# A hybrid decoder layer on one core: attention sums placed between gate units, and weight loads scheduled first

## The chip, the cores and the metric

The kernel runs on one core of a Trainium2 chip, as one launch. The metric is device time in microseconds (us), the median of several runs. Engines are named as the profile does: PE (matrix multiplies), PEld (its weight loads), DVE (vector), ACT (scalar), POOL (GpSimd) and SP (which issues nearly all DMAs here).

## The reference, cut to what matters

One decoder layer over 1024 tokens of width 1024, all in float32. The part around the change:

```python
proj = h @ w_in                        # q, k, v of mLSTM and attention, gates
# attention: 3 groups (dilations 1, 4, 16), 8 heads each; outs and log-denominators
wts = jax.nn.softmax(jnp.stack(lses, axis=0), axis=0)
y_b = jnp.sum(wts[..., None] * jnp.stack(outs, axis=0), axis=0)
g_a, g_b = jnp.split(jax.nn.sigmoid(gate_pre), 2, axis=-1)
merged = g_a * (y_a @ w_proj_a) + g_b * (y_b @ w_proj_b)
x = x + merged @ w_out
x = x + (jax.nn.silu(hf @ w_gate) * (hf @ w_up)) @ w_down
```

`y_b` is a sum over the three dilations; `gate_pre` is 2048 more columns of `proj`.

## The kernel before, in words

Every large product is done as three float32r products (high times high, high times low, low times high). A weight piece is loaded into a `raw` tile by `raw_piece` (L97 to L100; two `raw` buffers, 512 KB each), and `split` (L102) makes its high part on ACT (L103) and its low part on POOL (L104). The projections use a Strassen-like scheme with seven block products: `gemm_s` (L279) calls `w7`, which loads **two** raw pieces, the upper and the lower half of the rows, and forms the four sums S1 to S4 of them on DVE (L241 to L244); only the form A11 needs the first piece alone. The seven products P1, P7, P6, P5, P2, P4, P3 then run on PE (L263 to L265), 12 matmuls of 128x512 each, so 84 for a unit. The four output blocks leave PSUM through DVE (L294, and L668 in a gate unit), a gate unit's go through a tanh on ACT (L669) and are stored to DRAM (`gt_d`, L670) from one of two `e` tiles. P7 of the next unit needs the PSUM bank that L668 of this one empties.

After the projections and the recurrence of each head, the kernel comes to the part in question. `attn_combine` stores the softmax weights of the groups (`c_d`, L637). `attn_sum(i)` (L641, i = 0 to 3) makes `y_b`: for two halves and three groups, so six iterations, it loads the weights of two heads, each broadcast over 64 partitions (L649, two DMAs), and the group's numerators (L651), multiplies them on DVE (L652), adds (L654), and stores the half to `yb_d` (L657). All these tiles are `c` tiles, of which there are six. In all there are 24 iterations. `merge_b` (L967) then reads `yb_d` back (L963), splits it on ACT and POOL and multiplies it with `w_proj_b` (L184 to L186); `merge_a` goes on with `w_proj_a`.

The order of instructions on each engine, and in the DMA queue of SP, is not that of the code: a scheduler takes the program, gives each instruction a priority by its place in it, and fixes at build time in which row each engine works. Each engine then works through its row strictly in order, and SP waits at a DMA whose buffer or data is not ready, whatever stands behind. The place in the program is set by the list `ORDER` (L915): `m` are mLSTM heads, `a` attention pairs, `r` rows of denominators, `c` the combine, `g` gate units, `s` the four sums. Gate units 8 to 11 follow the sums there.

At the start of the kernel, SP loads eight tiles of x (L77) and, between the second and the third, the first two raw pieces. ACT sums their squares (L138), DVE scales them (L149), PE transposes them (L155).

Of the kernel before, what the change touches and what calls it, by code (L numbers as in the profile page):

```python
# [19 lines left out]
P = 128  # L20
# [19 lines left out]
def layer_kernel(ctx, tc, x, norm_mix_g, w_in, b_gate_if, conv_w, conv_b, mlstm_norm_g,  # L40
# [3 lines left out]
    ACT, DVE, POOL, PE, SP = nc.scalar, nc.vector, nc.gpsimd, nc.tensor, nc.sync  # L44
# [10 lines left out]
    def T(tag, shape, dt=F32):  # L55
        cnt[0] += 1
        return sb.tile(list(shape), dt, tag=tag, bufs=SBT[tag], name=f"{tag}{cnt[0]}")

    def PS(tag, shape=(P, 512)):
        cnt[0] += 1  # L60
        return ps.tile(list(shape), F32, tag=tag, bufs=PST[tag], name=f"p{tag}{cnt[0]}")
# [34 lines left out]

    def raw_piece(src, r0, nk, c0, ncol, tag="raw"):  # L97
        raw = T(tag, (P, nk, ncol))
        SP.dma_start(raw, src[r0:r0 + nk * P, c0:c0 + ncol].rearrange("(k p) c -> p k c", p=P))
        return raw  # L100

    def split(dh, dl, src):  # L102
        ACT.activation(dh, src, AF.Copy)  # L103
        POOL.tensor_tensor(dl, src, f(dh), op=ALU.subtract)  # L104

    raw0 = [raw_piece(w_in, kp * P, 4, C_VM + (NH - 1) * DH, 264) for kp in (0, 4)]
    for t in range(2, NT):
        load_x(t)
# [59 lines left out]
    def w_tiles(src, r0, K, c0):  # L168
        res = [(T("whi", (P, K, P), F32R), T("wlo", (P, K, P), F32R)) for _ in range(2)]
        for p in range(0, K, 4):  # L170
            raw = raw_piece(src, r0 + p * P, 4, c0, 256)
            for m in range(2):
                split(res[m][0][:, p:p + 4, :], res[m][1][:, p:p + 4, :], raw[:, :, m * P:(m + 1) * P])
        return res
# [14 lines left out]
    def gemm_h(src, r0, c0, ncol, K, stat, evac, raws=None, ts=range(NT), tags=(("whi", "wlo"),) * 2, quick=False):  # L189
        pieces = []  # L190
        for kp in range(0, K, 4):
            raw = raws[kp // 4] if raws else raw_piece(src, r0 + kp * P, 4, c0, ncol)
            wh, wl = (T(tg, (P, 4, ncol), F32R) for tg in tags[kp // 4])
            if quick:
                for ks, eng in ((slice(0, 2), DVE), (slice(2, 4), POOL)):
                    ACT.activation(wh[:, ks], raw[:, ks], AF.Copy)
                    eng.tensor_tensor(wl[:, ks], raw[:, ks], f(wh[:, ks]), op=ALU.subtract)
            else:
                split(wh, wl, raw)
            pieces.append((wh, wl))  # L200
        for t in ts:
            p = PS("mm", (P, ncol))
            for k in range(K):
                wh, wl = pieces[k // 4][0][:, k % 4, :], pieces[k // 4][1][:, k % 4, :]
                sh, sl = stat(k, t)
                PE.matmul(p, sh, wh, start=(k == 0), stop=False)  # L206
                PE.matmul(p, sh, wl, start=False, stop=False)
                PE.matmul(p, sl, wh, start=False, stop=(k == K - 1))
            evac(t, p)
# [702 lines left out]
        ACT.activation(hi, t1s[k], AF.Copy)  # L912
        DVE.tensor_tensor(lo, t1s[k], f(hi), op=ALU.subtract)

    ORDER = "m0 a00 a01 r0 m1 a10 a11 r1 m2 a20 a21 r2 c m3 g0 g1 g2 g3 s0 s1 s2 s3 g8 g9 g10 g11".split()  # L915
    mlstm_gates()
    mlstm_v2(0)
    for g in range(3):
# [21 lines left out]

    for step in ORDER:
        if step[0] == "a":
# [233 lines left out]
    for B in range(NS // BK):  # L1176
# [15 lines left out]
        for cg in range(2):  # L1192
            def wpiece(half, m, tags):

                c0 = cg * 512 + m * 256
                rows = w_down[B * BK * 256:(B + 1) * BK * 256, c0:c0 + 256].rearrange("(k i p) c -> i p k c", i=2, p=P)[half]
                res, k0 = [], 0
                for tg, nk in tags:
                    t_ = T(tg, (P, nk, 256))
                    SP.dma_start(t_, rows[:, k0:k0 + nk, :])  # L1200
                    res.append((t_, slice(k0, k0 + nk)))
                    k0 += nk
                return res
            a11, a21 = wpiece(0, 0, [("raw", BK)]), wpiece(0, 1, [("raw", BK)])
            a22, a12 = wpiece(1, 1, [("u", 2), ("u", 1)]), wpiece(1, 0, [("u", 2), ("u", 1)])
            s1, s2 = T("sm", (P, BK, 256)), T("sm", (P, BK, 256))
# [75 lines left out]
    for c in range(2):  # L1282
        wd.append([])
        for k0 in range(0, K4, 2):
            raw = T("raw", (P, 2, 512))
            r0 = (2 * NS + k0) * P
# [13 lines left out]
    for t in range(NT):  # L1300
        ssq, sd = small(2), small(1)
        for c in range(2):
            p = PS("mm")
# [61 lines left out]
```

## Time and profile before

| what | value |
|---|---|
| median of 3 runs | 2164.43 us (2159.92 to 2174.46) |
| the profiled execution | 2172.26 us |
| its span, first to last instruction | 2170.3 us |
| PE busy | 2033.1 us, 94% of the span |
| POOL, DVE, ACT busy | 965.0, 1355.7, 811.3 us |
| mean granted clock of PE | 0.974 of full |

The profile is of one execution, and the times in its rows are microseconds from the start of the span. "Busy" counts the time in which an engine works at an instruction. The bracket at the end of a row of the timeline is the idle time of that engine ahead of the row, and what ended it. Names of tiles are shown without their numbers there (`raw<-in_w_in` is a load of a piece of `w_in` into a raw tile).

### The profile page before, as it was taken

The page shows a single profiled execution, that of the slowest core. Times are in us where ns is not written, and L with a number is a line of the kernel's source. Part 1 is how long each engine was busy: PE and PEld are TensorE (multiplying, and loading weights), DVE is VectorE, ACT ScalarE, POOL GpSimd, SP SyncE. Part 2 cuts the span into 40 slices and gives each one's busy share as a digit, 9 for nine tenths or more (in the row PEclk, how much of TensorE's full clock was granted, in tenths as well). Part 3 has the DMA queues.
Part 4 walks back from the last instruction along what each step waited for, and adds up shares of the span by engine and source line. Part 5 has one row for each costly group of instructions (what it writes and reads, how often), then busy time and mean ns, then how long its engine had stood idle before and what let it go on. Part 6 is the DMA issues. An engine that isn't in the chain of part 4 may idle for free. (4 is left out here: it accounts for less than half of the span.)

```text
span 2170.3 us, 31051 instructions
## 1 busy us (share of the span) xinstructions
PE 2033.1 (94%) x11209; PEld 1695.8 (78%) x11209; DVE 1355.7 (62%) x2329; ACT 811.3 (37%) x1726; POOL 965.0 (44%) x727
## 2 busy tenths in 40 slices
PE   6999999999999999999874999998999999998998
PEld 6999877777777677877763778896788888888996
DVE  7832267666776688668664574439665555576676
ACT  5322243344333344345422422345233332344323
POOL 4444443312433233314322747455545454567770
PEclk9999999999999999999996999999999999999999
DMA  4342443434344444444377576654332333374422
GB/s 150 100 120 87 109 132 118 143 106 145 115 134 122 127 142 127 147 160 148 107 222 233 174 233 220 235 177 145 107 116 91 100 102 101 119 241 146 148 71 88
DMA packets 247972, 304.38 MB, mean 140 GB/s; under 512 B 33817, under 2 KB 170540, under 8 KB 247820
## 3 DMA queue, kind: packets, MB, share of 16 engines
q1 hardware_dynamic: 246524, 300.19, 44.2%
q10 hardware_dynamic: 1296, 2.23, 0.3%
q8 instruction: 88, 1.44, 0.3%
q14 instruction: 64, 0.52, 0.1%
HBM read 208.13 MB, written 94.22 MB: 139 GB/s over the span
## 5 line engine op out<-in xcount | busy, mean ns | idle before, releaser
L104 POOL TENSOR_TENSOR wlo<-sm,whi 128x512 fp32r<-128x512 f32 (+1 forms) x260 | 365.9, 1419 | 583.8 <-ACT whi L103 550.6
L104 POOL TENSOR_TENSOR wlo<-raw,whi 128x512 fp32r<-128x512 f32 (+3 forms) x228 | 342.7, 1517 | 357.0 <-ACT whi L103 345.9
L263 PE MATMUL pmm<-h,whi 128*128 128x512 f32 x824 | 335.9, 408 | 15.7 <-ACT u L293 7.6
L264 PE MATMUL pmm<-h,whi 128*128 128x512 f32 x824 | 332.5, 404 | 0.8 <-DVE h L228 0.8
L265 PE MATMUL pmm<-h,wlo 128*128 128x512 f32 x824 | 332.8, 404 | 0.0
L103 ACT ACTIVATE whi<-sm 128x512 fp32r<-128x512 f32 (+1 forms) x260 | 159.1, 635 | 276.7 <-PE pmm L264 140.1
L263 PE MATMUL pmm<-t,whi 128*128 128x512 f32 x504 | 203.7, 404 | 44.7 <-ACT whi L103 36.8
L103 ACT ACTIVATE whi<-raw 128x512 fp32r<-128x512 f32 (+3 forms) x228 | 146.9, 671 | 234.8 <-issue 66.7
L263 PEld LDWEIGHTS pmm<-h,whi 128*128 128x128 f32 x824 | 159.6, 194 | 61.6 <-ACT u L293 10.7
L264 PE MATMUL pmm<-t,whi 128*128 128x512 f32 x504 | 203.7, 404 | 0.0
L265 PE MATMUL pmm<-t,wlo 128*128 128x512 f32 x504 | 203.5, 404 | 0.0
L264 PEld LDWEIGHTS pmm<-h,whi 128*128 128x128 f32 x824 | 158.5, 192 | 39.5 <-issue 4.0
L265 PEld LDWEIGHTS pmm<-h,wlo 128*128 128x128 f32 x824 | 157.5, 191 | 37.8 <-issue 2.5
L241 DVE TENSOR_TENSOR sm<-raw,raw 128x512 f32<-128x512 f32 x58 | 44.5, 767 | 181.5 <-DMA raw<-in_w_gate 60.5
L263 PEld LDWEIGHTS pmm<-t,whi 128*128 128x128 f32 x504 | 97.0, 193 | 69.3 <-ACT whi L103 37.2
L782 DVE SCALAR_TENSOR_TENSOR c<-c,pm__329,c 128x256 f32<-128x256 f32 x192 | 117.3, 652 | 14.9 <-ACT c L780 13.8
L580 ACT ACTIVATE s<-s,nm 128x128 f32<-128x128 f32 (+1 forms) x192 | 84.6, 443 | 103.6 <-DVE nm L575 52.4
L264 PEld LDWEIGHTS pmm<-t,whi 128*128 128x128 f32 x504 | 96.2, 191 | 22.6 <-issue 1.5
L265 PEld LDWEIGHTS pmm<-t,wlo 128*128 128x128 f32 x504 | 95.9, 190 | 22.8 <-issue 2.3
L206 PE MATMUL pmm<-whi,h 128*128 128x256 f32 (+1 forms) x224 | 63.5, 290 | 9.3 <-DVE ifp L391 4.1
L553 PE MATMUL pS<-c,c 64*128 64x128 f32 (+1 forms) x384 | 72.2, 348 | 0.0
L293 ACT ACTIVATE u<-pmm 128x512 f32<-128x512 f32 x54 | 31.9, 590 | 86.6 <-PE pmm L265 86.6
(526 smaller groups left out, 5088.2 us busy)
## 6 DMA issues: line engine op xcount, KB each, us to landing
raw<-in_w_in SPq DMA_DIRECT2D x74, 512.0 KB
gt_d<-e SPq DMA_DIRECT2D x48, 256.0 KB
raw<-in_w_gate SPq DMA_DIRECT2D x24, 512.0 KB
raw<-in_w_up SPq DMA_DIRECT2D x24, 512.0 KB
raw<-in_w_out SPq DMA_DIRECT2D x16, 512.0 KB
va_d<-u SPq DMA_DIRECT2D x24, 256.0 KB
s<-gt_d SPq DMA_DIRECT2D x24, 256.0 KB
qa_d<-e SPq DMA_DIRECT2D x24, 256.0 KB
```

The source lines that it names most:

```text
L103: ACT.activation(dh, src, AF.Copy)
L104: POOL.tensor_tensor(dl, src, f(dh), op=ALU.subtract)
L206: PE.matmul(p, sh, wh, start=(k == 0), stop=False)
L241: DVE.tensor_tensor(s1, a21, a22, op=ALU.add)
L263: PE.matmul(bank, wh[:, k, :], bh, start=start and k == 0, stop=False, skip_group_check=True)
L264: PE.matmul(bank, wh[:, k, :], bl, start=False, stop=False, skip_group_check=True)
L265: PE.matmul(bank, wl[:, k, :], bh, start=False, stop=k == 3, skip_group_check=True)
L293: ACT.activation(u2, ba, AF.Copy)
L553: PE.matmul(sps[a][:, o:o + w], qT[a * 64:(a + 1) * 64, qt % 4 * P:(qt % 4 + 1) * P], kT[a * 64:(a + 1) * 64, (b0 - kt0) * P:(b0 - kt0) * ...
L580: ACT.activation(s[:, o:o + w], s[:, o:o + w], AF.Exp, bias=nm[:, qt, c:c + 1], accum_out=ll[:, qt, c:c + 1])
L782: DVE.scalar_tensor_tensor(y[:, m, :], xr[:, m, j:j + 256], cw[:, kt, j:j + 1], y[:, m, :], op0=ALU.mult, op1=ALU.add)
```

## The change

It has two edits. The DMA of `raw_piece` is issued under the scheduler's first priority, ahead of all that has none; and in `ORDER` each sum follows one of the gate units 0 to 3.

```diff
     def raw_piece(src, r0, nk, c0, ncol, tag="raw"):
         raw = T(tag, (P, nk, ncol))
-        SP.dma_start(raw, src[r0:r0 + nk * P, c0:c0 + ncol].rearrange("(k p) c -> p k c", p=P))
+        with tc.high_priority():
+            SP.dma_start(raw, src[r0:r0 + nk * P, c0:c0 + ncol].rearrange("(k p) c -> p k c", p=P))
         return raw
...
-    ORDER = "m0 a00 a01 r0 m1 a10 a11 r1 m2 a20 a21 r2 c m3 g0 g1 g2 g3 s0 s1 s2 s3 g8 g9 g10 g11".split()
+    ORDER = "m0 a00 a01 r0 m1 a10 a11 r1 m2 a20 a21 r2 c m3 g0 s0 g1 s1 g2 s2 g3 s3 g8 g9 g10 g11".split()
```

Below are rows of the built programs, in which a tile has its number. The numbers of `c` tiles and of tiles in gate units 1 to 3 differ between the two programs because the sums are written elsewhere; those of gate units 8 to 11 are the same in both, and line numbers from L99 on are one higher in the changed program.

The first place is in SP's row, at the second raw piece of gate unit 9 (`raw_10642`). Before, behind the last of the 24 iterations:

```order
L657 DMA yb_d_326<-c_10457 128x512
L651 DMA c_10484<-num_d_304 128x512
L649 DMA c_10490<-c_d 64x512 x2
L651 DMA c_10491<-num_d_308 128x512
L670 DMA gt_d<-e_10587 128x512
L670 DMA gt_d<-e_10604 128x512
L99 DMA raw_10642<-in_w_in 128x4x256
L963 DMA c_11076<-yb_d_323 128x512
```

Now, in the fifth iteration:

```order
L671 DMA gt_d<-e_10452 128x512
L650 DMA c_9931<-c_d 64x512 x2
L100 DMA raw_10642<-in_w_in 128x4x256
L658 DMA yb_d_323<-c_9905 128x512
L652 DMA c_9932<-num_d_301 128x512
L650 DMA c_9938<-c_d 64x512 x2
L652 DMA c_9939<-num_d_305 128x512
```

It has moved ahead of the loads of some 19 iterations; the later pieces up to the first of `w_proj_b` now also stand among them.

The second place is on DVE, where gate unit 8 empties two PSUM banks (`e_10620` after P4, `e_10636` after P3) that unit 9 needs for P7 and P5. Before:

```order
L652 TENSOR_TENSOR c_10484<-c_10483,c_10484 128x512
L654 TENSOR_TENSOR c_10478<-c_10478,c_10484 128x512
L652 TENSOR_TENSOR c_10491<-c_10490,c_10491 128x512
L668 TENSOR_TENSOR e_10620<-pmm_10531,u_10532 128x512
L654 TENSOR_TENSOR c_10478<-c_10478,c_10491 128x512
L668 TENSOR_TENSOR e_10636<-pmm_10574,u_10532 128x512
L241 TENSOR_TENSOR sm_10644<-raw_10640,raw_10642 128x512
```

Now:

```order
L653 TENSOR_TENSOR c_10110<-c_10109,c_10110 128x512
L653 TENSOR_TENSOR c_10116<-c_10115,c_10116 128x512
L669 TENSOR_TENSOR e_10620<-pmm_10531,u_10532 128x512
L655 TENSOR_TENSOR c_10110<-c_10110,c_10116 128x512
L669 TENSOR_TENSOR e_10636<-pmm_10574,u_10532 128x512
L653 TENSOR_TENSOR c_10123<-c_10122,c_10123 128x512
```

They stood behind the multiplication of the 24th iteration and stand now behind that of the 11th. Those of the units 9 and 10 follow in the same way: unit 9's four behind the 14th, 15th, 16th and 18th iteration, unit 10's behind the 21st, 22nd, 24th and 24th.

The third place is the start of SP's row, with the first tiles of x (`t_68`, `t_69`, `t_70`) and the first two weight pieces (`raw_84`, `raw_86`). Before:

```order
L77 DMA t_68<-in_x 128x1024
L85 DMA s_77<-in_norm_mix_g 8x128
L77 DMA t_69<-in_x 128x1024
L99 DMA raw_84<-in_w_in 128x4x264
L99 DMA raw_86<-in_w_in 128x4x264
L77 DMA t_70<-in_x 128x1024
```

Now:

```order
L100 DMA raw_84<-in_w_in 128x4x264
L100 DMA raw_86<-in_w_in 128x4x264
L77 DMA t_68<-in_x 128x1024
L85 DMA s_77<-in_norm_mix_g 8x128
L77 DMA t_69<-in_x 128x1024
L77 DMA t_70<-in_x 128x1024
```

The two weight pieces, 528 KB each, now go ahead of the first two tiles of x. With it the rows of the first 90 us or so stand in another order on PE, ACT and DVE. Elsewhere only a few rows change places, by one or two.

## Rows read from the trace of the kernel before

**Rows 1.** The page: busy time, then tenths of 40 slices of 54 us.

```profile
PE 2033.1 (94%) x11209; PEld 1695.8 (78%) x11209; DVE 1355.7 (62%) x2329; ACT 811.3 (37%) x1726; POOL 965.0 (44%) x727
...
PE   6999999999999999999874999998999999998998
...
DMA  4342443434344444444377576654332333374422
```

**Rows 2.** Windows: length, busy PE PEld DVE ACT POOL, clock, DMA share, GB/s.

```profile
1090.00:1120.00 30.00, 25.96 (x117) 21.25 (x115) 17.52 (x43) 9.02 (x18) 9.11 (x7) 1.00 0.76 232
1120.00:1150.00 30.00, 12.21 (x44) 9.55 (x44) 18.13 (x38) 3.20 (x5) 0.00 (x0) 0.67 0.78 245
1150.00:1180.00 30.00, 10.14 (x34) 8.13 (x35) 10.93 (x15) 4.71 (x8) 8.07 (x6) 0.59 0.89 283
1180.00:1210.00 30.00, 28.76 (x123) 22.77 (x122) 12.55 (x17) 12.07 (x21) 14.27 (x12) 1.00 0.33 107
```

**Rows 3.** Waits of PE, whole span: us in total, times, longest us.

```profile
PE pmm L263 <- ACT whi L103: 38.2, 4, 36.8
```

**Rows 4.** Timeline of PE: start, us, instruction, idle before.

```profile
1120.85 0.79 PE L263 MATMUL pmm<-t,whi 128*128 128x512 f32 x1 [4.89 <-DVE u L294]
...
1169.86 0.79 PE L263 MATMUL pmm<-t,whi 128*128 128x512 f32 x1 [36.79 <-ACT whi L103]
...
1174.67 0.40 PE L264 MATMUL pmm<-h,whi 128*128 128x512 f32 x1
...
1180.25 0.40 PE L265 MATMUL pmm<-t,wlo 128*128 128x512 f32 x1
...
1230.96 0.39 PE L184 MATMUL pmm<-t,whi 128*128 128x512 f32 x1
```

**Rows 5.** Timeline of SP, around the sums.

```profile
1105.65 1.09 SPq L649 DMA_DIRECT2D c<-c_d  x2
1106.79 0.59 SPq L657 DMA_DIRECT2D yb_d<-c  x1
...
1160.66 0.39 SPq L99 DMA_DIRECT2D raw<-in_w_in  x1
```

**Rows 6.** Timelines of POOL and DVE: the raw tiles of units 8 and 9.

```profile
1099.56 3.50 POOL L104 TENSOR_TENSOR wlo<-raw,whi 128x512 fp32r<-128x512 f32 x2 [1.55 <-ACT whi L103]
...
1167.85 0.69 DVE L241 TENSOR_TENSOR sm<-raw,raw 128x512 f32<-128x512 f32 x1 [2.02 <-DMA raw<-in_w_in]
```

**Rows 7.** Timeline of DVE: iterations 5, 7 and 24 of the sums, then L668.

```profile
1112.57 0.69 DVE L652 TENSOR_TENSOR c<-c,c 128x512 f32<-128x512 f32 x1 [4.90 <-DMA c<-num_d]
...
1116.84 0.66 DVE L652 TENSOR_TENSOR c<-c,c 128x512 f32<-128x512 f32 x1
...
1163.29 0.69 DVE L652 TENSOR_TENSOR c<-c,c 128x512 f32<-128x512 f32 x1 [1.07 <-DMA c<-num_d]
1163.93 0.69 DVE L668 TENSOR_TENSOR e<-pmm,u 128x512 f32<-128x512 f32 x1
```

**Rows 8.** DMA issues from 1080 to 1180 us: count, KB each.

```profile
c<-c_d SPq DMA_DIRECT2D x48, 128.0 KB
c<-num_d SPq DMA_DIRECT2D x24, 256.0 KB
gt_d<-e SPq DMA_DIRECT2D x8, 256.0 KB
```

**Rows 9.** Timelines of ACT, DVE and PE at the start of the kernel.

```profile
8.08 1.09 ACT L103 ACTIVATE whi<-raw 128x1056 fp32r<-128x1056 f32 x1 [0.32 <-DMA raw<-in_w_in]
9.58 1.08 ACT L103 ACTIVATE whi<-raw 128x1056 fp32r<-128x1056 f32 x1 [0.41 <-DMA raw<-in_w_in]
...
8.59 3.63 DVE L149 TENSOR_SCALAR t<-t,small 128x1024 f32<-128x1024 f32 x2
...
16.65 1.42 DVE L149 TENSOR_SCALAR t<-t,small 128x1024 f32<-128x1024 f32 x2
...
30.88 2.68 PE L155 MATMUL pPT<-cs,t 128*128 128x128 f32 x8 [4.08 <-DVE t L149]
```

## The prediction, made before the changed kernel ran

> **What bounds the kernel now.** I read the page first, then windows, then PE's waits and timeline, then the row of the engine that each wait names. By the page PE is busy for 94% of the span, and no other engine for more than 62%; the slices show that its idle time isn't spread out, but lies mostly in slices 20 to 22 (8, 7, 4 tenths), just where the DMA line rises to 7 [rows 1]. So PE is the bound, and there is one hole. In windows of 30 us it is busy for 25.96, 12.21, 10.14 and then again 28.76 us, and its clock falls to 0.67 and 0.59 in the two bad ones [rows 2]. The reader is to see in the waits that this is one event: 38.2 us of waiting for the high part of a weight form, of which 36.8 in one piece [rows 3], ahead of the matmul at 1169.86 [rows 4]. This is P7 of gate unit 9. Following it back: DVE makes the sums of that unit's two raw pieces at 1167.85, after a wait for a raw load [rows 6], and SP issued that load at 1160.66 [rows 5], since it stood behind the loads of all 24 iterations of the sums. Its buffer wasn't the reason: POOL had read the last of the raw tile that it replaces by 1099.56 + 3.50 = 1103.06 [rows 6]. A second chain had ended no sooner: L668 of unit 8, which empties the bank for P7, stood behind the 24th multiplication (1163.29) and ran at 1163.93 [rows 7].
>
> **The change, part by part.**
>
> *The load goes forward, and so does L668.* SP now issues the piece right after the broadcasts of the fifth iteration, which end at 1105.65 + 1.09 = 1106.74 [rows 5]; 54 us earlier. From issue to the DVE sum it took 7.2 us under a DMA share of 0.89 [rows 2, 5, 6], so it is there by 1114. PE works on without a hole until 36.79 us before 1169.86, that is until 1133.07 [rows 4], 19 us later. L668 follows the 11th iteration instead of the 24th, and at the present pace (below) that is at 1116.84 + 4 x 2.73 = 1128. So P7 is ready on both sides: **-36.8 us**. The idle time has a second price. The 11 matmuls from 1169.86 to 1174.67 start 0.437 us apart, the 24 from there to 1180.25 start 0.2325 us apart [rows 4]; after the hole PE runs at 1.2 GHz, later at 2.4. Without it these 11 cost 11 x 0.205 = **-2.3 us**. Gross: -39.1.
>
> *The sums now run beside PE's work, not in its hole, and they pace it.* DVE's row mixes them with the evacuations of units 9 and 10: unit 10's four stand behind iterations 21 to 24. From iteration 7 to 24 there are 17 steps in 1163.29 - 1116.84 = 46.45 us, 2.73 each [rows 7]. What would PE want? From 1133.1 it has six products of unit 9 (6 x 12 x 0.2325 = 16.7), unit 10 (84 x 0.2325 = 19.5) and P1 of unit 11 (2.8); then at 1172.1 P7 of unit 11 needs unit 10's bank, behind iteration 24. That allows (1172.1 - 1116.84) / 17 = 3.25 us a step. At the present 2.73 the sums would cost nothing. But they get company. A step moves 2 x 128 + 256 KB and a third of a 256 KB store [rows 8], 597 KB, so 17 of them 10.4 MB. Into the same stretch now come five raw pieces of 512 KB, ten gate stores and about six further loads and stores of 256 KB, 6.8 MB. At the 283 GB/s of the busiest window [rows 2] the 17.2 MB take 61 us, to 1177.6: 5.5 us late. The lower bound is 0 (DMA keeps up), the upper takes the 245 GB/s of the window before it [rows 2]: 70 us, 15 late. I take the row with the highest share, since the DMA queue will now always have work: **+5**.
>
> *On DVE ahead of that.* The four sums of unit 9 (L241 to L244, 0.69 each as at 1167.85 [rows 6]) now come ahead of L294 of unit 8, for which PE already waited 4.89 us [rows 4]: +2.8 at most, but DVE waited 4.90 us for iteration 5's load just there [rows 7], which covers most of it. Between 0 and 2.8 I take **+1**.
>
> *What is late next: the product with w_proj_b.* It began at 1230.96 [rows 4], 67 us behind the last iteration, and its inputs had time. Now y_b is complete at about 1178, and PE is through with unit 11 at 1172.1 + 5 + 16.7 = 1194, 16 us later. Between lie the reload (about 7 us, as for the raw load above) and eight splits on POOL, each 128x512 like those of [rows 6], 3.50 / 2 = 1.75 us, so 14: if none of them ran beside the loads, 21 us. Between 0 and +5 I take **+1**, since all but the last of the eight halves are written, and can be read back, before the last iteration ends.
>
> *The start.* The first two tiles of x now land after two pieces of 528 KB. ACT could begin with the second of these 9.58 - 8.08 = 1.5 us after the first, and waited for its load [rows 9], so two pieces delay x by 3 us. Against it, the pair of scalings on DVE took 3.63 us beside POOL's splits and 1.42 without [rows 9]; the splits now run before. PE's wait at 30.88, 4.08 us for the scaling of the last four tiles [rows 9], may also get shorter, as ACT is rid of the splits sooner. Between -4 and +3 I take 0.
>
> Sum: -39.1 + 5 + 1 + 1 = **-32 us**. Against the profiled execution (2172.26 us, its span 2170.3) that is 2140; that execution lies 7.8 us above the median of the runs, and the forecast for the median is 2164.4 - 32 = **2132 us**.
>
> By the Trainium skill, DMA: Bandwidth & Descriptors, section Issuing engines are not separate DMA queues, all transfers share the same 16 DMA engines and interleave with each other; so a weight load put first takes its time from the sums rather than adding to what the engines can do. The shares of 0.76 to 0.89 in the hole [rows 2] agree with that, and it is the case for the first rival below; by it alone, with those shares squeezed into the shorter stretch, most of the +5 to +15 would be paid.
>
> **The rivals.**
>
> *DMA binds the stretch.* For it: the share was 0.78 and 0.89 with PE idle [rows 2], and raw pieces and gate stores come on top. Against it: the last 0.11 to 0.22 of the engines' time was still free, and GB/s rose with the share. The sums at 4.1 us a step cost 15, and the product with w_proj_b 5 more as y_b comes late: -39 + 15 + 1 + 5 = -18, 2146.
>
> *Nothing takes the place of the hole.* The steps stay at or below 3.25 us, and the start gains: -39 - 3 = -42, 2122. For it: 2.73 us now.
>
> *The sums hold DVE, and PE behind it, for longer than the hole did (slower).* Place: L668 of units 8 to 10 in DVE's row. A step then costs what the slowest one showed: 4.90 us of waiting and 1.4 of multiply and add [rows 7], 6.3. The 24th comes at 1116.84 + 17 x 6.3 = 1223.9, 52 us after 1172.1; -39 + 52 + 1 = +14, 2178. It turns to a loss from 3.25 + 38 / 17 = 5.5 us a step. Against it: a step of 5.5 us moves 109 GB/s, far under any of the windows [rows 2].
>
> *The load doesn't really move:* SP would wait at it for its buffer and hold up the sums too; 2164. Against it the buffer's last reader at 1103 [rows 6].
>
> **How the numbers follow.** Forecast, with sums 0 to 9 us late: 0.55, from 2120 to 2146 by its own terms. DMA binds: 0.22. Nothing takes its place: 0.15. Slower: 0.04. Doesn't move, or is given back where I don't see it: 0.04. The range for 8 in 10 goes from 2118 (nothing takes its place, and the start gains its 4) to 2154 (DMA binds, and a median that can lie some us off: the three runs before span 14.5). A measurement of this kernel tells about 1%, 21.6 us, from no change, so the bound is 2142.8: the forecast lies below it in most of its range, the case with no new wait wholly, the case that DMA binds mostly not. That makes 0.72 faster, 0.24 the same, 0.04 slower.
>
> **What would show it right or wrong.** The wait of 36.8 us is gone from PE's list, and the raw load of unit 9 is issued near 1107. PE's windows from 1120 to 1180 show over 25 of 30 us, with a clock near 1.00. If the sums pace PE, DVE's L652 steps take over 3.25 us, and PE shows waits of some us each ahead of P7 or P5 of units 10 and 11, for DVE L668 or L294. If y_b is late, PE waits ahead of the first L184. The forecast is wrong if a wait of over 15 us stands at any of these, or if the first 90 us get longer by more than 3.

## The result, and the profile after

The changed kernel takes **2139.39 us** in the median of four runs (2132.07 to 2141.57); the kernel before took 2168.34 us (four runs, 2159.92 to 2174.46: the three from above and one of 2172.24). The ratio is 0.9864, with a 95% interval from 0.9841 to 0.9887: 29 us faster, where 32 were forecast. The profiled executions stand at 2172.26 and 2139.01 us, 33.25 apart, the spans at 2170.3 and 2137.0. The profiled execution of the kernel before lies 3.9 us above that kernel's median, the other one at its own; so some 4 of the 33 us that are taken apart below may belong to this one execution and not to the change. Line numbers from L99 on are one higher now (L263 is L264, L294 is L295, L668 is L669).

The page of the changed kernel, with the three lines that answer to [rows 1]:

```profile
PE 2034.5 (95%) x11209; PEld 1699.2 (80%) x11209; DVE 1348.8 (63%) x2329; ACT 811.0 (38%) x1726; POOL 971.4 (45%) x727
...
PE   6999999999999999999888899998999999999998
...
DMA  4243344443444434554368876653333333375422
```

PE's dip to 4 tenths is gone; in its place four slices stand at 8. The same in windows of 30 us, as in [rows 2]:

```profile
1090.00:1120.00 30.00, 24.50 (x107) 19.73 (x106) 17.45 (x41) 8.31 (x16) 9.22 (x7) 0.96 0.83 253
1120.00:1150.00 30.00, 25.43 (x99) 19.58 (x98) 24.53 (x43) 9.66 (x16) 10.18 (x7) 0.90 0.84 266
1150.00:1180.00 30.00, 27.92 (x110) 22.15 (x110) 14.82 (x22) 10.64 (x18) 12.38 (x10) 0.92 0.84 248
1180.00:1210.00 30.00, 25.93 (x103) 20.05 (x101) 18.34 (x18) 15.99 (x29) 25.42 (x19) 0.94 0.76 241
```

PE's waits over the whole span, where the 36.8 us of [rows 3] stood at the head; the wait for the high part of a weight form is now 1.8 us:

```profile
PE pPT L881 <- DVE num L875: 13.5, 5, 6.8
PE pmm L264 <- DVE u L295: 10.2, 4, 4.8
...
PE pmm L264 <- DVE e L669: 4.2, 2, 3.0
...
PE pmm L264 <- ACT whi L104: 1.8, 3, 1.1
```

Before, PE waited 7.8 us in three for L294 and never for L668; so the waits for L669 are new, and those for L295 are more. In PE's timeline they stand here (P4 of unit 8; P7 and P4 of unit 9; P4 of unit 10; P7 of unit 11), and the last row is the start of the product with w_proj_b, which doesn't wait:

```profile
1119.22 0.79 PE L264 MATMUL pmm<-t,whi 128*128 128x512 f32 x1 [4.80 <-DVE u L295]
...
1133.16 0.50 PE L264 MATMUL pmm<-t,whi 128*128 128x512 f32 x1 [1.14 <-DVE e L669]
...
1147.52 0.50 PE L264 MATMUL pmm<-t,whi 128*128 128x512 f32 x1 [2.94 <-DVE u L295]
...
1170.94 0.50 PE L264 MATMUL pmm<-t,whi 128*128 128x512 f32 x1 [2.08 <-DVE u L295]
...
1184.16 0.50 PE L264 MATMUL pmm<-t,whi 128*128 128x512 f32 x1 [3.02 <-DVE e L669]
...
1203.40 0.39 PE L185 MATMUL pmm<-t,whi 128*128 128x512 f32 x1
```

What L295 and L669 wait for is seen in DVE's timeline (the first row is the first sum of unit 9's pieces; L653 are iterations 7 and 24 of the sums):

```profile
1110.41 0.69 DVE L242 TENSOR_TENSOR sm<-raw,raw 128x512 f32<-128x512 f32 x1 [4.23 <-DMA raw<-in_w_in]
...
1119.09 0.68 DVE L653 TENSOR_TENSOR c<-c,c 128x512 f32<-128x512 f32 x1
...
1142.07 0.69 DVE L242 TENSOR_TENSOR sm<-raw,raw 128x512 f32<-128x512 f32 x1 [3.29 <-DMA raw<-in_w_in]
...
1146.79 0.67 DVE L295 TENSOR_TENSOR u<-u,pmm 128x512 f32<-128x512 f32 x1
...
1166.81 1.68 DVE L242 TENSOR_TENSOR sm<-raw,raw 128x512 f32<-128x512 f32 x1 [2.83 <-DMA raw<-in_w_in]
...
1170.22 0.67 DVE L295 TENSOR_TENSOR u<-u,pmm 128x512 f32<-128x512 f32 x1
...
1182.83 0.68 DVE L653 TENSOR_TENSOR c<-c,c 128x512 f32<-128x512 f32 x1
1183.43 0.68 DVE L669 TENSOR_TENSOR e<-pmm,u 128x512 f32<-128x512 f32 x1
```

L295 stands behind the sums of the next unit's pieces, and these wait for a raw load; L669 of unit 10 stands behind the 24th multiplication, as L668 of unit 8 did before.

**Where the 33.3 us come from.** PE's work can be cut at two marks that both kernels have: P4 of unit 8 (6013 matmuls lie ahead of it) and the first matmul with w_proj_b (285 matmuls further, 4913 ahead of the end). Windows between the marks, the kernel before:

```profile
0.00:1120.85 1120.85, 1069.33 (x6013) 871.46 (x6013) 732.28 (x1429) 440.06 (x1062) 395.23 (x336) 0.98 0.43 130
1120.85:1230.96 110.11, 71.06 (x285) 56.26 (x285) 48.09 (x75) 33.04 (x58) 41.47 (x31) 0.80 0.64 204
1230.96:2170.30 939.34, 892.69 (x4913) 768.03 (x4911) 575.35 (x826) 338.16 (x607) 528.29 (x361) 0.98 0.45 145
```

and the changed one:

```profile
0.00:1119.22 1119.22, 1068.76 (x6013) 873.21 (x6013) 727.61 (x1426) 441.11 (x1063) 399.77 (x337) 0.98 0.43 131
1119.22:1203.40 84.18, 73.91 (x285) 57.73 (x285) 52.07 (x77) 31.83 (x55) 41.38 (x31) 0.91 0.83 257
1203.40:2137.00 933.60, 891.86 (x4913) 768.26 (x4911) 569.13 (x828) 338.07 (x608) 530.25 (x360) 0.98 0.45 146
```

Up to the first mark -1.6, between the marks -25.9, behind the second -5.7. So the total was forecast well for a reason that is only three quarters of it: between the marks, where all of it was expected but the +1 for P4 of unit 8 (-39.1 + 5 + 1 + 1 = -32), 6 us less came, and 7.4 us came from where none was forecast. The experiments ask what moved the load (the two edits apart), what the rest between the marks is, and where the other 7.4 are from.

### The profile page after: what moved, and what is told of

The parts are those of the page before. It is cut to its first block, busy times and chain, and to the rows that moved or that the text cites. A ratio compares the mean times of both kernels' runs of the same rounds, so it can differ in the third digit from the quotient of the medians.

```text
span 2137.0 us, 31055 instructions
## 1 busy us (share of the span) xinstructions
PE 2034.5 (95%) x11209; PEld 1699.2 (80%) x11209; DVE 1348.8 (63%) x2329; ACT 811.0 (38%) x1726; POOL 971.4 (45%) x727
## 5 line engine op out<-in xcount | busy, mean ns | idle before, releaser
L105 POOL TENSOR_TENSOR wlo<-sm,whi 128x512 fp32r<-128x512 f32 (+1 forms) x260 | 370.3, 1435 | 537.8 <-ACT whi L104 511.7
L264 PE MATMUL pmm<-h,whi 128*128 128x512 f32 x824 | 333.6, 405 | 13.3 <-DVE c L1147 4.7
L264 PE MATMUL pmm<-t,whi 128*128 128x512 f32 x504 | 204.8, 406 | 14.3 <-DVE u L295 9.8
L264 PEld LDWEIGHTS pmm<-h,whi 128*128 128x128 f32 x824 | 158.5, 192 | 58.2 <-ACT whi L104 9.2
L242 DVE TENSOR_TENSOR sm<-raw,raw 128x512 f32<-128x512 f32 x58 | 45.7, 788 | 175.4 <-DMA raw<-in_w_gate 61.1
L264 PEld LDWEIGHTS pmm<-t,whi 128*128 128x128 f32 x504 | 97.3, 193 | 40.1 <-DVE u L295 12.3
L783 DVE SCALAR_TENSOR_TENSOR c<-c,pm__329,c 128x256 f32<-128x256 f32 x192 | 115.9, 645 | 17.2 <-ACT c L781 16.3
L207 PE MATMUL pmm<-whi,h 128*128 128x256 f32 (+1 forms) x224 | 65.8, 301 | 8.6 <-DVE ifp L392 4.3
L209 PE MATMUL pmm<-whi,h 128*128 128x256 f32 (+1 forms) x224 | 65.2, 303 | 4.0 <-DVE h L161 3.3
```

What stands on the lines that cost most here:

```text
L242: DVE.tensor_tensor(s1, a21, a22, op=ALU.add)
L264: PE.matmul(bank, wh[:, k, :], bh, start=start and k == 0, stop=False, skip_group_check=True)
L783: DVE.scalar_tensor_tensor(y[:, m, :], xr[:, m, j:j + 256], cw[:, kt, j:j + 1], y[:, m, :], op0=ALU.mult, op1=ALU.add)
```

## The experiments

Each is measured against the kernel before on the same chip; edits are against the changed kernel unless said otherwise. "A step" is the time from iteration 7 to iteration 24 of the sums by DVE's timeline, divided by 17; the changed kernel has 3.75 us, (1182.83 - 1119.09) / 17.

**One edit at a time.** The priority alone, with the step list of before:

```
-    ORDER = "... c m3 g0 s0 g1 s1 g2 s2 g3 s3 g8 g9 g10 g11".split()
+    ORDER = "... c m3 g0 g1 g2 g3 s0 s1 s2 s3 g8 g9 g10 g11".split()
```

> Only the first priority of the weight loads; the step list stands as before (all four sums behind g3). Theory A (the priority does all of it): the raw load of unit 9 goes ahead of the sums, and the schedule that follows from it also puts the evacuation of unit 8 and the sums of unit 9 ahead of the 24th multiplication, so the same 29 us are gained as by the whole change: 2139, within 5. Theory B (both edits are needed, the sums hold the evacuation of unit 8 on DVE otherwise): P7 of unit 9 still waits for the 24th multiplication, near 1164, and only 4 to 8 us are gained: 2160.

Measured: 2141.33 us, ratio 0.9878 (0.9854 to 0.9902), span 2137.2 against 2137.0. Between the marks 84.33 us, where the change has 84.18. And the new step list alone, without the priority:

```
-        with tc.high_priority():
-            SP.dma_start(raw, src[r0:r0 + nk * P, c0:c0 + ncol].rearrange("(k p) c -> p k c", p=P))
+        SP.dma_start(raw, src[r0:r0 + nk * P, c0:c0 + ncol].rearrange("(k p) c -> p k c", p=P))
```

> Only the new step list (s0 to s3 between the g), loads without priority. Theory A: nothing, the raw load of unit 9 is issued behind the loads of all 24 iterations as before, and PE's wait of some 37 us stands: 2168, within 5. Theory B: the sums are spread, the evacuation of unit 8 comes earlier and the load of unit 9 goes in between; at least 10 of the 37 us are gone: 2158 or less.

Measured: 2168.99 us, ratio 1.0002 (0.9987 to 1.0016). PE's longest wait is still there, in its list of waits:

```profile
PE pmm L263 <- ACT whi L103: 39.0, 4, 37.6
```

Theory A holds on both sides: the priority does all of it, the step list nothing. By the names of tiles without their numbers, the rows of SP and DVE have the order of the kernel before with the list alone, and that of the changed kernel with the priority alone, from the first to the last: between the gate units, the place in the list moves nothing (ahead of m3 it does, as is seen below). And the load's priority also moves L669, which it doesn't name: with the load early, the scheduler puts the products and evacuations of unit 9 early too.

**The start.** The first two pieces without priority:

```
-    raw0 = [raw_piece(w_in, kp * P, 4, C_VM + (NH - 1) * DH, 264) for kp in (0, 4)]
+    raw0 = [raw_piece(w_in, kp * P, 4, C_VM + (NH - 1) * DH, 264, "raw", False) for kp in (0, 4)]
```

> The change, but the first two pieces (raw0, the load ahead of x) have no priority. Theory A: the start is a wash, as predicted (0, between -4 and +3), and the total stays at 2139 within 3; PE's wait at the first transposes goes back from 8.0 to 5.3 us, and the waits for the scalings of x come back. Theory B: the 1.6 us by which the changed kernel is ahead before the sums come from there, and 2 to 4 us are lost: 2142.

Measured: 2137.24 us, ratio 0.9851 (0.9830 to 0.9872): not to be told from the change. PE's first wait is back at 5.0 us from 8.0, and PE comes to P4 of unit 8 at 1116.07, 3.2 us ahead of the changed kernel. A's figures came and B's didn't: the changed kernel's lead of 1.6 us there doesn't come from the first two pieces. But the start isn't a wash either. Here is one matmul behind the reordered rows of the start, first in the kernel before, then in the changed one:

```profile
87.70 0.27 PE L726 MATMUL pPV<-cs,g_c 128*32 128x128 f32 x1
```

```profile
91.01 0.27 PE L727 MATMUL pPV<-cs,g_c 128*32 128x128 f32 x1
```

In the kernel measured here it stands at 87.63. In all four kernels with plain first pieces it stands between 87.63 and 88.52, in the ten that load them first between 89.28 and 91.10. So loading them first costs PE some 1 to 3 us; the changed kernel starts 3.3 us behind.

It makes most of this good at one place, some 500 us on. PE waits there for L823 (L824 in the changed kernel), which stands in DVE's row behind the sums of a raw piece. The kernel before, PE and DVE:

```profile
591.97 2.92 PE L840 MATMUL pS<-c,c 128*128 128x256 f32 x8 [3.54 <-DVE st L823]
```

```profile
587.84 0.69 DVE L241 TENSOR_TENSOR sm<-raw,raw 128x512 f32<-128x512 f32 x1 [3.73 <-DMA raw<-in_w_in]
```

The changed one:

```profile
594.77 1.57 PE L841 MATMUL pS<-c,c 128*128 128x256 f32 x8 [1.53 <-DVE st L824]
```

```profile
591.70 0.69 DVE L242 TENSOR_TENSOR sm<-raw,raw 128x512 f32<-128x512 f32 x1 [2.81 <-issue]
```

PE's wait is 2.0 us shorter, and behind it the granted clock is 1.00 (594.77 to 600.13), where it was 0.64 before (591.97 to 600.05). The stretch of 40 matmuls around it (584.80 to 600.05 in the kernel before) takes 15.3 us there, 15.0 with the step list alone, and 10.3 to 12.1 in all twelve kernels with the priority. The changed kernel enters it 4.8 us later than the kernel before and leaves it 0.1 later; the 1.6 us of lead come behind it. So this gain is the priority's once more, at another unit.

**What the rest between the marks is.** Fewer bytes for as many instructions: each broadcast of coefficients brings 32 columns.

```
-                                 bass.AP(..., ap=[[0, 64], [1, 512]]))
+                                 bass.AP(..., ap=[[0, 64], [1, 32]]))
...
-                DVE.tensor_tensor(nu, cb, nu, op=ALU.mult)
+                DVE.tensor_tensor(..., cb[:, None, 0:32].to_broadcast([P, 16, 32]), ..., op=ALU.mult)
```

> The change, but each broadcast of the coefficients brings 32 columns in place of 512, and the multiplication uses these 32 for all columns (the sums so lose most of their coefficients): as many instructions, waits and buffers, but a step of the sums moves some 355 KB in place of 597. Theory A (DMA's bytes pace the stretch): DMA share there falls from 0.83 to about 0.55, a step of the sums takes 2.2 to 2.8 us in place of 3.75, and the waits of unit 9 to 11 (10 us, and some 5 of half clock) mostly go: 2124 to 2130. Theory B (the order of DVE and the few buffers pace it, not bytes): steps stay above 3.3 us, the waits ahead of P4 and P7 stay, the time within 4 of 2139.

Measured: 2149.11 us, ratio 0.9906 (0.9890 to 0.9921): 10 us slower than the change, which neither theory said. A step did fall, to (1166.62 - 1115.92) / 17 = 2.98 us. The window from iteration 7 to 24, first in this kernel, then in the changed one:

```profile
1115.92:1166.62 50.70, 31.44 (x116) 24.23 (x116) 38.26 (x62) 12.01 (x21) 16.73 (x12) 0.78 0.67 208
```

```profile
1119.09:1182.83 63.74, 55.27 (x212) 42.97 (x212) 43.02 (x69) 20.31 (x34) 24.91 (x18) 0.91 0.85 261
```

But with the smaller loads the scheduler built another row for SP: two stores of gates now stand behind the loads of iteration 24, here in SP's timeline of this kernel:

```profile
1161.71 0.53 SPq L652 DMA_DIRECT2D c<-num_d  x1
1162.29 0.90 SPq L671 DMA_DIRECT2D gt_d<-e  x2
```

Until they have gone out, both `e` tiles are full (DVE had filled them by 1148.1), L669 can't empty a bank, and PE waits. A second chain ended no sooner: in DVE's row the next L669 stands behind the 24th multiplication (1166.62), and it ran without idle time ahead of it. DVE's row, then PE's:

```profile
1167.23 1.28 DVE L669 TENSOR_TENSOR e<-pmm,u 128x512 f32<-128x512 f32 x2
```

```profile
1168.06 0.76 PE L264 MATMUL pmm<-h,whi 128*128 128x512 f32 x1 [15.81 <-DVE e L669]
```

This is the old hole again, with stores in the place of the load, and again with an evacuation behind the last iteration: the places that the scheduler gave a few instructions cost more than what 40% fewer bytes a step saved. Whether the stores alone would have done it wasn't tried.

Then four edits that relieve one engine or buffer each and leave the sums' bytes as they are. The gates' stores go from SP to ACT's queue:

```
-            SP.dma_start(gt_d[i0 + m, :, n * 512:(n + 1) * 512], t_)
+            ACT.dma_start(gt_d[i0 + m, :, n * 512:(n + 1) * 512], t_)
```

> The change, with the stores of the gates (L671) issued by ACT behind its tanh in place of SP. Theory A (a row of SP or DVE that stands at one late instruction is what is left to pay): SP no longer stops at a store for ACT's tanh ahead of the loads behind it, DVE L669 no longer waits for a store that stands behind the sums' loads; 2 to 6 us of the waits ahead of P4 and P7 of units 9 to 11 go: 2133 to 2137. Theory B (DMA's bytes pace the stretch): the bytes are the same, so is the time: 2139 within 3.

Measured: 2136.44 us, ratio 0.9853 (0.9838 to 0.9869), a step 3.65 us. That lies in both theories' ranges, and its interval overlaps that of the change: taken alone it decides nothing. The sums of the pieces on POOL:

```
-        DVE.tensor_tensor(s1, a21, a22, op=ALU.add)
+        eng.tensor_tensor(s1, a21, a22, op=ALU.add)
...
+        gemm_s(w_in, c0, Bq, gate_evac(i0), eng=POOL if i >= 8 else DVE)
```

> The change, with the four sums of the raw pieces (L242 to L245) of units 8 to 11 on POOL in place of DVE. Theory A (order on DVE): the additions L295, for which P4 waits, no longer stand behind sums that wait for a raw load; PE's waits of 2.9 and 2.1 us ahead of P4 of units 9 and 10, and the half clock behind them, go: 2132 to 2136, if POOL, busy for some 41 of 84 us there, takes 3 x 4 more pieces of 1.3 us. Theory B (the raw loads come late because DMA is busy): the wait moves from DVE's row to POOL's and PE waits as long ahead of P7 and P6: 2139 within 3, or slower.

Measured: 2143.97 us, ratio 0.9895 (0.9874 to 0.9916), a step 3.67 us. Theory B: POOL now waits for the raw load (at L242, idle for 10.65 us up to 1110.19; the row names no releaser, but in the changed kernel this sum starts at 1110.41 on the load), and PE waits no less; ahead of P4 of unit 8 it has become twice as long, since DVE's row holds L295 behind another late load of the sums (6.06 us of waiting up to 1111.37) and behind five instructions of 128x4 that take some 1.2 us each; in the changed kernel four of these five take 0.15 to 0.17 us. PE's row, one of the five, and POOL's row beside it:

```profile
1122.59 0.79 PE L264 MATMUL pmm<-t,whi 128*128 128x512 f32 x1 [9.46 <-DVE u L295]
```

```profile
1118.41 1.20 DVE L870 TENSOR_SCALAR l_t<-l_t 128x4 f32<-128x4 f32 x1
```

```profile
1118.32 1.26 POOL L105 TENSOR_TENSOR wlo<-raw,whi 128x512 fp32r<-128x512 f32 x1
```

Each of the five ends 0.02 to 0.03 us behind an instruction of POOL, this one at 1119.61 behind 1119.58. So the edit also holds up DVE beside POOL's added work; that is read from the rows.

One load in place of the two broadcasts of a step:

```
-                for a in range(2):
-                    SP.dma_start(cb[a * 64:(a + 1) * 64, :], bass.AP(..., ap=[[0, 64], [1, 512]]))
+                SP.dma_start(cb, bass.AP(..., ap=[[S, 2], [0, 64], [1, 512]]))
```

> The change, with the two broadcast loads of a step (64 partitions each) made one load of 128 partitions: the same bytes, 24 fewer issues on SP at 0.54 us. Theory A: a step of the sums gets some 0.3 us shorter, 3.4 in place of 3.75, near what PE leaves free, and 2 to 5 us are gained: 2134 to 2137. Theory B (bytes): 3.75 stays, 2139 within 3.

Measured: 2214.4 us, ratio 1.0217 (1.0198 to 1.0236): a big miss of both theories. A step takes 7.10 us, (1261.5 - 1140.8) / 17, in a window of a low share, with the same bytes to move; and SP itself is held, an issue lasting up to several us (window of this kernel, then a row of SP's timeline):

```profile
1140.80:1261.50 120.70, 64.32 (x201) 47.97 (x200) 42.22 (x66) 19.49 (x34) 24.04 (x18) 0.74 0.41 139
```

```profile
1133.56 3.55 SPq L650 DMA_DIRECT2D c<-num_d  x1
```

So this load is slow by its shape, not by its bytes. The Trainium skill, DMA: Bandwidth & Descriptors, section Rules for kernel authors, says that an outermost dimension smaller than 16 confines a transfer to at most that many engines; here it is 2, in the two loads that it replaces 64. The low share agrees with that; no row here shows single engines. It is also the only kernel of the study in which the predicted slower case came true: above 5.5 us a step, it said, the sums cost more than the hole did, and at the place that it named: PE waits 41.5 us for the evacuation L667 (L669 in the changed kernel) and 33.5 us for L295 between 1100 and 1290.

The coefficients in the two `pt` buffers, so that the six `c` hold products alone:

```
-                cb, nu = T("c", (P, 512)), T("c", (P, 512))
+                cb, nu = T("pt", (P, 512)), T("c", (P, 512))
```

> The change, with the broadcast coefficients in the two buffers pt in place of the six c, which then hold products and accumulators alone, so that more steps are in flight. Theory A (few buffers): loads are issued earlier, a step of the sums falls to 3.3 us or less, 3 to 6 us are gained: 2133 to 2136. Theory B (bytes): the DMA share is at 0.83 already, the steps stay at 3.6 or more and the time within 3 of 2139.

Measured: 2143.55 us, ratio 0.9883 (0.9867 to 0.9899), a step 3.67 us. From iteration 7 on, a load of numerators is now issued 12.3 us ahead of its multiplication in the mean, 5.7 us in the changed kernel; so more loads are in flight, and the pace is the same. That is theory B for the pace; the time lies 1.6 us above its range.

**Another place for the sums.** All four ahead of m3 in the step list, then two of them:

```
-    ORDER = "... c m3 g0 s0 g1 s1 g2 s2 g3 s3 g8 g9 g10 g11".split()
+    ORDER = "... c s0 s1 s2 s3 m3 g0 g1 g2 g3 g8 g9 g10 g11".split()
...
+    ORDER = "... c s0 s1 m3 g0 s2 g1 s3 g2 g3 g8 g9 g10 g11".split()
```

> The change, with the four sums named in the step list ahead of m3 in place of between the g: their loads and multiplications get a higher rank than mLSTM head 3 and the gate units, and their row in DVE's and SP's order lies one to two gate units earlier. Theory A (the bytes of sums, raw pieces and stores in one stretch pace PE): the same company in the new place, so the steps still take 3.5 us or more there, but y_b is done earlier and the stretch ahead of the product with w_proj_b is thinner: 2132 to 2139. Theory B (the sums take the c buffers from head 3's core): PE waits more for the convolution (L786) and the scores of head 3, and 5 or more us are lost: 2144 or more.

Measured: 2153.43 us, ratio 0.9930 (0.9904 to 0.9956). The sums lie 100 us earlier, and from iteration 7 to 24 they take (1082.07 - 1021.75) / 17 = 3.55 us a step, at the highest share of all:

```profile
1021.75:1082.07 60.32, 51.41 (x204) 39.48 (x204) 39.38 (x53) 18.48 (x32) 22.09 (x17) 0.94 0.91 270
```

The same pace with other company, as A said; but the time is B's, and for another reason than B gave. After 6225 matmuls PE still stands where it does in the changed kernel (1185.14 against 1184.16), after 6453 it is 13 us behind (1258.46 against 1245.44): it waits 11 us between 1180 and 1240, where no sums run beside head 3's end and the last gate units, for evacuations on ACT and DVE most of all.

> The change, with s0 and s1 ahead of m3 and s2 and s3 behind g0 and g1 in the step list: two batches of 12 steps with two gate units between them. Theory A (bytes in one stretch pace PE): the DMA share falls below 0.75 in the windows of the first batch and rises in the second; of the 10 us of waits and 5 us of half clock half goes: 2130 to 2136. Theory B (last batch late): the second 12 steps end where the 24th ends now or later, the product with w_proj_b waits for y_b, and nothing is gained: 2139 or more.

Measured: 2139.89 us, ratio 0.9871 (0.9842 to 0.9899): as the change. After 6013 matmuls PE is 3.0 us behind it (1122.26), and the 285 up to the second mark take 78.97 us, 5.2 less. Half the sums early moved waits, and saved none that the time shows.

**Both small gains together**, the first pieces plain and the stores on ACT:

> The change, with both edits that came out a little faster: the first two pieces without priority, and the gates' stores issued by ACT. If the two gains (2.1 and 2.9 us under the change by their medians, 2 to 4 us by their profiled spans) are real and add up: 2133 to 2135. If they are within what the measurement tells apart: 2137 to 2139.

Measured: 2132.26 us (2131.13 to 2132.87), ratio 0.9834 (0.9808 to 0.9860), a step 3.60 us, 80.99 us between the marks. It is the fastest version that computes the whole, some 7 us under the change by the medians; the two intervals still overlap (the change's begins at 0.9841), so that lead is likely, not certain.

**The sums left out**, to measure what they still cost:

```
-                DVE.tensor_tensor(nu, cb, nu, op=ALU.mult)
...
+            acc = T("c", (P, 512))
+            SP.dma_start(acc, nums_d[0][i][:, sl])
             SP.dma_start(yb_d[i][:, sl], acc)
```

> The change without the sums: each y_b half is the numerator of the first dilation alone, loaded once and stored (24 multiplications, 16 additions, 48 broadcasts and 16 of the 24 loads are left out; some 12 of 14 MB). This measures the mis-sized term: what the sums still cost beside PE's work. Theory A (the sums' bytes still hold up PE by 12 to 17 us, waits and half clock together): the DMA share of the stretch falls below 0.5, the waits ahead of P4 and P7 of units 9 to 11 go, 2122 to 2128. Theory B (these waits belong to the gate units' own chain of load, sum and split, with or without the sums): they stay, 2134 to 2139.

Measured: 2121.81 us, ratio 0.9792 (0.9776 to 0.9808), 17.6 us under the change, just below the range of A. (By the sizes of [rows 8] 10.5 MB are left out, not 12.) The window of this kernel between the marks (its 286th matmul is one that began just ahead):

```profile
1114.16:1181.45 67.29, 65.83 (x286) 52.72 (x285) 25.15 (x40) 32.28 (x57) 39.43 (x31) 1.00 0.47 147
```

The 285 matmuls take 67.3 us here, 84.2 in the change and 110.1 before. So in the change the sums cost 16.9 us between the marks: 8.8 of idle time (84.18 - 73.91 against 67.29 - 65.83) and 8.1 of matmuls at the lower clock (73.91 against 65.83 busy, granted clock 0.91 against 1.00). Ahead of the first mark they cost another 5.1 (1119.22 against 1114.16), P4's wait of 4.80 most of all; behind the second this kernel gives 4.1 back (937.72 us against 933.60), for a reason that is left open. And the gate units' own chain of load, sum and split costs next to nothing: the waits ahead of P4 and P7 are gone with the sums.

## Why the prediction was right, and where it was not

- *The load goes forward, 36.8 us of waiting go.* Right in every part. The load of unit 9 is issued at 1105.40 (forecast 1106.7), its DVE sum runs at 1110.41 (by 1114), L669 of unit 8 no longer stands behind the 24th multiplication. What the prediction didn't know is that one of the two edits does all of this (ratios 0.9878 and 1.0002).
- *The half clock behind the hole, -2.3 us.* It went there and came back elsewhere. The lower clock was charged to the old wait and not to the new ones: PE is busy for 71.06 us between the marks before, for 73.91 now, for 65.83 without sums. The windows from 1120 to 1180 show a clock of 0.90 and 0.92, where the prediction looked for one near 1.00. Behind each of the waits of 2.94, 2.08 and 3.02 us, eight matmuls start 0.42 us apart in place of 0.23, at a granted clock of 0.50 (1148.10 to 1151.48), 0.51 and 0.50: the lower of PE's two clocks, 1.2 GHz. A sum that puts several short waits in the place of a long one has to charge each with its own slow matmuls.
- *The sums pace PE, +5.* This is the step that failed, by its size: "I take the row with the highest share, since the DMA queue will now always have work". The bytes were right (17.2 MB forecast, 63.74 us at 261 GB/s are 16.6), the rate was not: 261 GB/s, not 283, at a share of 0.85. With 261 the working gives 17.2 MB / 261 GB/s = 66 us, so iteration 24 at 1182.8, 10.7 late and not 5.5. It stood at 1182.83; iteration 7 came 2.25 us later than assumed and the steps took less than 66 us, so that this fits so well is partly luck. Together with the clock, the terms +5, +1 and +1 became 13.2 us (39.1 - 25.9). In PE's own account the missing 6 us are mostly clock: the forecast took 29.8 us of idle time away and 2.3 of busy time, and measured are 28.8 of idle time less (110.11 - 71.06 = 39.05 before, 84.18 - 73.91 = 10.27 now) and 2.9 of busy time more. As the sums set when P7 of unit 11 may start, the two terms can't be priced apart. That the bytes are the larger part of what sets the pace is borne out by the five kernels in which SP, DVE, buffers or the place were changed and a step stayed at 3.55 to 3.67 us, and by the one with fewer bytes, 2.98. They aren't all of it: that one's window moved 50.70 us x 208 GB/s = 10.5 MB, which at 261 GB/s would have taken 40 us.
- *The first rival, DMA binds the stretch*, gave 4.1 us a step and -18 in all; measured are 3.75 and -25.9 between the marks. The truth lay between it and the forecast. (The shares that the prediction gives for the hole hold a window ahead of it, 0.76; the hole's own are 0.78 and 0.89.)
- *DVE ahead of that, +1.* Unit 8's P4 waits 4.80 us, before 4.89 [rows 4]: 0. The mechanism came true one unit later: L295 of units 9 and 10 stands behind sums that wait for a raw load, 2.94 and 2.08 us.
- *y_b is late, +1.* No: the product with w_proj_b starts at 1203.40 without a wait.
- *The start, 0.* It cost 3.3 us (91.01 against 87.70), outside the range of -4 to +3, and "the first 90 us get longer by more than 3" was one of the prediction's own signs of being wrong. The delay of x by two pieces was sized well (PE's first wait is 8.0 us, before 5.3); the shorter scalings that were to make up for it didn't. That PE is 1.6 us ahead at the first mark all the same is luck, as far as the prediction goes: it comes from the place near 590 us and from smaller ones behind it.
- *Nothing behind the sums*: the prediction had no term there, and 5.7 us came. Of these 4.2 lie in the down-projection, from 1914.06 and 1884.92 on, where both kernels' engines have the same rows in the same order; the next section but one shows them. The other 1.6 are spread over 700 us.

So 2139 lies some 7 us above 2132: 3.9 because the kernel before has its median at 2168.34 with the fourth run, and not at 2164.43, and 3.1 because the change gave 29 us and not 32. That these 3 aren't 6 is luck: a term that was 6 us too small met gains elsewhere that were not forecast, 7 us of them in the profiled executions.

## What to carry to other kernels

A hole of this kind is a matter of one instruction's place in a row that is worked strictly in order: look for the DMA or evacuation that stands behind a batch it doesn't need, give that one priority, and test each edit of a pair alone. When the batch then runs beside PE's work, price it with the rate that the traffic reaches in company, not with the best window, and charge the lower clock after each short wait. Before fewer bytes or fewer issues are counted as a gain, look at the row that the scheduler builds from them (10 us lost with 40% fewer bytes a step) and at the shape of the load (75 us lost with one in place of two).

## What was not expected of the hardware

An addition of two SBUF tiles on DVE, 128x512, which takes 0.69 us in the median of its line, took **10.54 us** in the down-projection of the kernel before. POOL's timeline there (two rows of it with no gap in POOL's work between them, then the first after its pause), DVE's and PE's:

```profile
1973.74 1.32 POOL L1186 TENSOR_TENSOR t<-e,t 128x512 fp32r<-128x512 f32 x1
...
1981.87 1.83 POOL L104 TENSOR_TENSOR wlo<-raw,whi 128x768 fp32r<-128x768 f32 x1
1987.31 1.83 POOL L104 TENSOR_TENSOR wlo<-sm,whi 128x768 fp32r<-128x768 f32 x1 [3.61 <-ACT whi L103]
```

```profile
1973.70 10.54 DVE L1216 TENSOR_TENSOR sm<-raw,u 128x512 f32<-128x512 f32 x1 [2.31 <-issue]
```

```profile
1985.06 0.55 PE L1239 MATMUL pmm<-whi,h 128*128 128x256 f32 x1 [5.94 <-DVE t L1247]
```

DVE ends at 1984.24, 0.54 us after POOL has run out of work (1981.87 + 1.83), and PE pays 5.94 us. In the changed kernel the same instruction, with the same neighbours:

```profile
1944.57 1.28 POOL L1187 TENSOR_TENSOR t<-e,t 128x512 fp32r<-128x512 f32 x1
1945.82 2.61 POOL L105 TENSOR_TENSOR wlo<-u,whi 128x512 fp32r<-128x512 f32 x2
```

```profile
1944.66 1.75 DVE L1217 TENSOR_TENSOR sm<-raw,u 128x512 f32<-128x512 f32 x1 [2.44 <-issue]
```

Here DVE gets in when the first of POOL's instructions ends (1945.85), POOL's next takes longer, and PE's wait in this place is 2.78 us, for POOL. The Trainium skill, SBUF — State Buffer, section SBUF: two separate sides, says that a DVE instruction with two SBUF inputs and a GpSimd instruction that reads SBUF exclude each other for a whole instruction. The second pair of rows agrees; the first goes further and shows that a waiting DVE instruction can lose against POOL's whole unbroken row. It came in both kernels without the priority (10.54 and 10.42 us, the second with the step list alone) and in none of the twelve with it (the longest was 1.9). What decides it is open. The rows on either side have the same order, and the offset between them doesn't tell it: with the step list alone DVE starts 0.09 us behind POOL's instruction (1974.58 and 1974.49) and is held for 10.42 us, and the changed kernel has the same 0.09. That it is worth the 4.2 us found there wasn't tried. Both executions that show it lie 4 us above their kernel's median (2172.26 against 2168.34, 2173.01 against 2168.99), so others of the same kernels may be without it.
